# Modulation's sums on VectorE, k outermost in two first projections, and the residual's rows spread over the first expert

## The chip, the cores and the metric

The kernel runs on one core of a Trainium2 chip. The metric is the device time of one execution in microseconds (us). A time is the median of a few runs. One execution was also taken with the hardware profiler; its trace gives the rows shown below.

The engines: TensorE (PE; PEld is its loading of weights), VectorE (DVE), ScalarE (ACT), GpSimd (POOL), and SyncE (SP), which here issues nearly all of the transfers.

## The reference

The program computes two layers over 256 latent tokens of width 1024, with 256 context tokens beside the first layer. Everything is in fp32.

```
mods = split(silu(c) @ ada_w[i] + ada_b[i], 6)            # 6 vectors of 1024 per layer: the modulation
u = h * (1 + mods[1]) + mods[0]
layer 0: y = [neighbourhood attention | bidirectional SSD] (u) @ w_out
layer 1: y = short gated convolution (u)
h = LayerNorm(alpha * h + mods[2] * y) * ln_g + ln_b
f = channel(h * (1 + mods[4]) + mods[3])                  # layer 0: dense SwiGLU, layer 1: top-2-of-8 experts
h = LayerNorm(alpha * h + mods[5] * f) * ln_g + ln_b
```

The six modulation vectors of a layer are one row times a 1024 x 6144 matrix: 4 MB of weights for each vector of 1024, and little arithmetic. For the context tokens only the first two vectors of layer 0 are used.

## The kernel before

**Stages.** The program goes through the scan's projections, the scan and the values, z and its gate, attention (eight pairs of heads), the mixer's output projection, a norm and a turn (transposes that make u by feature), the dense feed-forward (22 tiles of features, then its output projection), a norm and a turn, the short convolution (8 tiles, then its output projection), the routing, and the eight experts with a final norm. An instruction's place in its engine's queue is fixed when the program is built: a scheduler orders each queue from a simulated timeline and the priorities of the program's order. `pinned` and `issue_after` put an instruction no earlier than the one named.

**Weights.** Every large weight comes as tiles of 1 MB (`raw`, L122, issued by SP) into a ring of buffers, whose number differs by stage. A granule of 1024 columns is split (`split`, L81): ScalarE copies the high part to fp32r (`whi`), VectorE subtracts to get the low part (`wlo`). A product is three fp32r matmuls: high x high, high x low, low x high (`mm3`, L90; `rows3`, L1245). A ring buffer is free when both parts of its two granules are made.

**Modulation.** `ada` (L242) is a generator that makes one or two vectors: it loads the weights, multiplies them on TensorE with `csil` (silu of c and of c_ctx, padded to 32 columns) as the stationary operand, four matmuls side by side in column groups of 32 (L258, plain fp32, two passes each), adds the bias, and turns the rows into columns (`modT`) or sends them through DRAM to all partitions (`gate`). For two vectors at a time a load is one k tile of 2048 columns; for one it is two k tiles of 1024. `background` (L99) hangs such generators onto the loads of a stage: after each `every` loads of the stage, `raw` lets the first task make one step, which is one load and its matmuls. Which vectors run where, layer/vector:

- z, attention and the mixer's output projection: 0/2 and 0/3, 0/4 and 0/5, half of 1/0 and 1/1, a step for every load (20 loads)
- ahead of the first norm: the other half of 1/0 and 1/1 (4 loads, `LEFT`)
- feed-forward: 1/2 and 1/3, and a quarter of 1/4, a step for every second load (9 loads)
- ahead of the second norm: the rest of 1/4 (3 loads, `REST`)
- routing: 1/5

**First projections.** After a turn, `ffn` (L835) and `short_conv` (L849) run `proj_T` for one output after the other: for each of the 8 k tiles of u the three matmuls, then the next output. The turn makes the k tiles of u one by one on ScalarE and VectorE.

**The residual's rows.** `keep_residual` (L822) writes alpha * (n * ln_g + ln_b) into h in eight VectorE steps of 512 columns. In the experts all eight are traced at once after the first expert's first product (L1342). n lies in the buffer `last`, and that buffer is one of the eleven of the experts' ring (L1455), so the load that falls to it waits for the last of these steps.

Of the kernel before, what the change touches and what calls it, by code (L numbers as in the profile page):

```python
# [7 lines left out]
F32 = mybir.dt.float32  # L8
# [4 lines left out]
OP = mybir.AluOpType  # L13
# [33 lines left out]
ONACT = ((0, 1), (1, 1))  # L47
LEFT = 4
X32 = 2
# [4 lines left out]
class Kernel:  # L54
# [43 lines left out]

    def background(self, tasks, every):  # L99

        self.tasks, self.every, self.loads = tasks, every, 0

# [19 lines left out]
    def raw(self, src, kk, cols):  # L122
        r = self.raw_tile()
        if not self.inside:
            self.loads += 1
            if self.loads % self.every == 0:
                self.inside = True
                self.step()
                self.inside = False
        v = r[:, :kk * cols].rearrange("p (k c) -> p k c", k=kk)  # L130
        self.nc.sync.dma_start(v, src)
        return v
# [48 lines left out]
    def constants(self):  # L181
        nc, io = self.nc, self.io
        c = self.const
        self.pad(c, 32)
        self.pad(self.work, 160)
        self.ident = c.tile([P, P], F32, name="ident")
        make_identity(nc, self.ident)
        self.ones = self.work.tile([P, P], F32, name="ones", bufs=1)
        nc.vector.memset(self.ones, 1.0)
        self.eps = c.tile([P, 1], F32, name="eps")  # L190
        nc.vector.memset(self.eps, EPS)
        self.ada_memory(self.work, 512)
# [48 lines left out]

    def ada(self, layer, m0, n, gates=(), cols=True, pin=False):  # L242

# [5 lines left out]
        bv = io["ada_b"][layer:layer + 1, c0:c0 + 4 * c].rearrange("a (j n) -> (a j) n", j=4)  # L249
        for r in range(2):  # L250
            nc.gpsimd.dma_start(self.ada_bias[r:r + 97:32, :c], bv)
        pa = self.ada_bank()
        kk = 512 // c
        for k0 in range(0, KT, kk):
            r = self.raw(w[:, k0:k0 + kk, c0:c0 + 4 * c], kk, 4 * c)
            for k in range(kk):
                for j in range(4):
                    nc.tensor.matmul(pa[32 * j:32 * j + 32, :c], self.csil[:, k0 + k, :], r[:, k, j * c:(j + 1) * c],  # L258
                                     start=(k0 + k == 0), stop=(k0 + k == KT - 1), tile_position=(0, 32 * j))
            yield k0  # L260
        rows = self.ada_rows[:, :c]
        done = nc.vector.tensor_add(rows, pa[:, :c], self.ada_bias[:, :c])
        if pin:
            self.pinned(done)
        if cols:
            pt = self.tmp()
            ns = c // P
            for s in range(ns):
                nc.tensor.transpose(pt[:, s * P:(s + 1) * P], rows[:, s * P:(s + 1) * P], self.ident)
            pv = pt[:, :c].rearrange("p (s j x) -> p s j x", s=ns, x=32)  # L270
            for r in range(2):
                nc.vector.tensor_copy(
                    self.modT[layer][:, r, m0 * KT:(m0 + n) * KT].rearrange("p (j s) -> p j s", s=ns),
                    pv[:, :, :, r].rearrange("p s j -> p j s"))
        if gates:
            flat = self.dram.tile([4, c], F32, name=f"gates{layer}{m0}")
            nc.gpsimd.dma_start(flat, rows[0:97:32, :])
            for m, dst in gates:
                j = (m - m0) * 4 // n
                nc.gpsimd.dma_start(dst, flat[j:j + 4 // n, :].rearrange("j n -> (j n)").partition_broadcast(P))  # L280

    def steps(self, task, n):
# [6 lines left out]
    def ada_memory(self, pool, c):  # L289
        self.ada_bias = pool.tile([P, c], F32, name="ada_bias", bufs=1)  # L290
        self.nc.gpsimd.memset(self.ada_bias, 0.0)
        self.ada_rows = pool.tile([P, c], F32, name="ada_rows", bufs=1)


# [49 lines left out]
    def proj_T(self, out, w, uh, ul, n, ks=range(KT)):  # L344

        for k in ks:
            self.mm3(out[:, :n], w[0][:, k], w[1][:, k], uh[:, k, :n], ul[:, k, :n], k == 0, k == KT - 1)
        return out[:, :n]

    def proj_tok(self, w, c0, n):  # L350
# [471 lines left out]
    def keep_residual(self, n, gb, factor):  # L822

        stt = self.nc.vector.scalar_tensor_tensor
        for i in range(NTT):
            for h in range(2):
                c = slice(h * 512, (h + 1) * 512)
                r = self.h[:, i, c]
                self.pinned(stt(r, n[:, i, c], factor, gb[:, 0, c], op0=OP.mult, op1=OP.mult))
                yield  # L830
                self.pinned(stt(r, gb[:, 1, c], factor, r, op0=OP.mult, op1=OP.add))
                yield


    def ffn(self, uh, ul, hh, hl, first, later):  # L835
        nc, io = self.nc, self.io
        ws = [self.by_feature(self.kpn(io[v][0]), 0, FFN, (t,)) for v, t in zip(("ffn_w1", "ffn_w3"), first)]
        for f in range(NF):
            p = self.acc("pf")
            for j in range(2):  # L840
                self.proj_T(p[:, j * T:], next(ws[j]), uh, ul, T)
            s = self.fp.tile([P, T], F32, name="fs", bufs=2)
            nc.scalar.activation(s, p[:, :T], AF.Silu)
            nc.vector.tensor_mul(s, s, p[:, T:])
            self.split(hh[:, f, :], hl[:, f, :], s)
# [3 lines left out]
    def short_conv(self, uh, ul, mh, ml, first, later):  # L849
# [3 lines left out]
        for ft in range(KT):  # L853
            p = [self.acc("pg"), self.acc("pg2")]
            reg = [p[0][:, :T], p[0][:, T:], p[1][:, :T]]
            for j in range(3):
                self.proj_T(reg[j], next(ws[j]), uh, ul, T)
            ci = self.fp.tile([P, T + 2], F32, name="sci", bufs=2)
# [15 lines left out]
    def front(self):  # L874
# [59 lines left out]
        for g in range(GROUPS):  # L934
# [3 lines left out]
        gp = self.pool("gates")  # L938
        gates = gp.tile([P, 2, D], F32, name="gates")
        gate = [gates[:, j, :] for j in range(2)]  # L940
        odd = self.ada(1, 0, 2, pin=True)
        self.background([self.ada(0, 2, 2, ((2, gate[0]),)), self.ada(0, 4, 2, ((5, gate[1]),)),
                         islice(odd, KT - LEFT)], 1)
        self.sh, self.sl = two(self.pool("mixs"), "mixs", KT)
# [9 lines left out]
        for half in range(2):  # L954
# [3 lines left out]
            nc.gpsimd.affine_select(out=wv[:, NKC:], in_=wv[:, NKC:], compare_op=OP.is_ge, fill=NEG,  # L958
                                    base=GW + 6 - NKC, pattern=[[-1, GW - NKC]], channel_multiplier=-1)
        self.attention()  # L960
        self.ready(AF.Sqrt, self.al[:, KT - 1, 0:1].bitcast(F32))
# [19 lines left out]
        self.residual_norm(accs, gate[0], n, ALPHA)  # L981
# [16 lines left out]
        first = [self.raw(w[:, :, j * D:j * D + 256], KT, 256) for j in (1, 2, 0)]  # L998
        self.residual_norm(accs, gate[1], n, 1.0)
# [315 lines left out]
    def experts(self):  # L1315
# [13 lines left out]
        for e in range(NE):  # L1329
            wu = [self.kpn(w[e]) for w in (w1, w3)]  # L1330
            wd = self.kpn(w2[e])
            po, last, x = None, None, xs[e % 2]
            for c, (c0, n) in enumerate(CHUNKS):
                def turned():
# [102 lines left out]
    def back_end(self):  # L1437
# [98 lines left out]
```

## Time and profile before

| | us |
|---|---|
| median of 3 runs | 1754.14 |
| fastest and slowest run | 1754.04, 1754.82 |
| the profiled execution | 1753.65 |
| its span (first to last instruction) | 1751.9 |
| TensorE, VectorE, ScalarE, GpSimd busy in the span | 1705.1, 1383.1, 1133.0, 119.1 |
| HBM read | 503.39 MB |

How to read the rows in this document. A row of a stretch reads: from and to in us, its length, then busy us and instructions of each engine that has any (PE, PEld, DVE, ACT, POOL in this order), the granted clock of TensorE, the busy share of the transfer engines, and GB/s. A row of the timeline reads: start, length in us, engine, line, operation, what it writes and what it reads, its shape, and how many were merged. A row of a group reads: line, engine, operation, tiles, shapes, count, then busy us and mean ns of one, then the idle time of the engine just before these and what ended most of it. A row of waits reads: who waited, for whom, us in total, times, the longest. Matmuls are pipelined, so that each one's record is longer than the distance to the next one's start.

### The profile page before, as it was taken

Reading aid. Unit: us, or ns where it says so; the run is one execution under the profiler, and the core shown is the slowest. Engines: PE = TensorE matmul, PEld = TensorE weight load, DVE = VectorE, ACT = ScalarE, POOL = GpSimd, SP = SyncE. Lnnn points to the kernel's source line nnn. Section 1 sums busy time; section 2 is a strip of 40 time slices with the busy share of each in tenths; the row PEclk is TensorE's granted clock in tenths of the full one; section 3 lists DMA queues with packets and bytes.
Section 4 is the critical chain, followed back from the end, with each engine's and each line's share of the span. In section 5 each row is a group of like instructions: output and inputs, shape, how many; then the busy total and the mean of one; then the engine's idle time right before and its main releaser. Section 6 shows DMA issues by size and latency. Waiting matters only on the chain. (4 is left out here: it accounts for less than half of the span.)

```text
span 1751.9 us, 25551 instructions
## 1 busy us (share of the span) xinstructions
PE 1705.1 (97%) x9400; PEld 1399.4 (80%) x9400; DVE 1383.1 (79%) x1784; ACT 1133.0 (65%) x1523; POOL 119.1 (7%) x241
## 2 busy tenths in 40 slices
PE   7999999999999999989999999999999999999996
PEld 5788776666999879768888888888888888888884
DVE  3697665555655567789998899998998998988987
ACT  3578554444444444468778877778777777777764
POOL 2036612110000010000000000000000000000000
PEclk9999999999999999999999999999999999999998
DMA  9346475358877585689999999999999999999991
GB/s 327 113 130 137 160 244 171 115 215 314 286 257 254 186 286 185 223 322 380 370 358 366 348 360 380 369 347 349 358 363 360 365 359 353 342 379 374 354 353 49
DMA packets 195358, 506.25 MB, mean 289 GB/s; under 512 B 9244, under 2 KB 79152, under 8 KB 191132
## 3 DMA queue, kind: packets, MB, share of 16 engines
q1 hardware_dynamic: 191504, 496.02, 77.8%
q0 software_dynamic: 3408, 8.44, 2.1%
q8 instruction: 75, 1.23, 0.3%
q14 instruction: 55, 0.45, 0.1%
q10 hardware_dynamic: 316, 0.12, 0.0%
HBM read 503.39 MB, written 1.14 MB: 288 GB/s over the span
## 5 line engine op out<-in xcount | busy, mean ns | idle before, releaser
L88 DVE TENSOR_TENSOR wlo<-wraw,whi 128x1024 fp32r<-128x1024 f32 x834 | 980.6, 1220 | 212.1 <-ACT whi L85 187.8
L85 ACT CAST whi<-wraw 128x1024 fp32r<-128x1024 f32 x834 | 840.1, 1054 | 347.5 <-PE bank L1251 74.5
L1250 PE MATMUL bank<-whi,x 128*128 128x512 f32 x896 | 349.3, 390 | 4.5 <-ACT whi L85 4.5
L1251 PE MATMUL bank<-whi,x 128*128 128x512 f32 x896 | 348.7, 390 | 0.0
L1253 PE MATMUL bank<-wlo,x 128*128 128x512 f32 x896 | 284.7, 392 | 3.6 <-DVE wlo L88 3.5
L1253 PEld LDWEIGHTS bank<-wlo,x 128*128 128x128 f32 x896 | 166.8, 188 | 42.7 <-DVE wlo L88 8.6
L1250 PEld LDWEIGHTS bank<-whi,x 128*128 128x128 f32 x896 | 168.1, 188 | 40.3 <-ACT whi L85 5.6
L1251 PEld LDWEIGHTS bank<-whi,x 128*128 128x128 f32 x896 | 168.1, 188 | 34.9
L1251 PE MATMUL bank<-whi,htl 128*128 128x512 f32 x440 | 171.5, 390 | 0.0
L1250 PE MATMUL bank<-whi,hth 128*128 128x512 f32 x440 | 171.5, 390 | 0.0
L1253 PE MATMUL bank<-wlo,hth 128*128 128x512 f32 x440 | 138.0, 395 | 0.0
L96 PE MATMUL pf<-ful,whi 128*128 128x256 f32 x352 | 100.0, 284 | 1.4 <-DVE ful L88 1.4
L95 PE MATMUL pf<-fuh,whi 128*128 128x256 f32 x352 | 100.6, 286 | 0.4 <-ACT fuh L85 0.4
L97 PE MATMUL pf<-fuh,wlo 128*128 128x256 f32 x352 | 99.4, 283 | 0.0
L1251 PEld LDWEIGHTS bank<-whi,htl 128*128 128x128 f32 x440 | 82.6, 188 | 17.6
L1250 PEld LDWEIGHTS bank<-whi,hth 128*128 128x128 f32 x440 | 82.6, 188 | 17.6
L95 PE MATMUL acc<-uh,whi 128*128 128x512 f32 (+1 forms) x256 | 92.1, 366 | 3.0 <-ACT whi L85 3.0
L1253 PEld LDWEIGHTS bank<-wlo,hth 128*128 128x128 f32 x440 | 80.0, 188 | 14.4
L96 PE MATMUL acc<-ul,whi 128*128 128x512 f32 (+1 forms) x256 | 91.4, 357 | 0.0
L97 PE MATMUL acc<-uh,wlo 128*128 128x512 f32 (+1 forms) x256 | 90.3, 353 | 0.0
L85 ACT CAST hth<-bank 128x512 fp32r<-128x512 f32 x56 | 32.3, 590 | 64.9 <-PE bank L1253 54.4
L95 PEld LDWEIGHTS pf<-fuh,whi 128*128 128x128 f32 x352 | 67.4, 192 | 7.8 <-issue 5.9
(372 smaller groups left out, 2505.0 us busy)
## 6 DMA issues: line engine op xcount, KB each, us to landing
wraw<-in_moe_w_dram SPq DMA_DIRECT2D x336, 1024.0 KB, 7.2
wraw<-in_ada_w_dram SPq DMA_DIRECT2D x40, 1024.0 KB, 5.2
wraw<-in_ffn_w_dram SPq DMA_DIRECT2D x32, 1024.0 KB, 6.1
wraw<-in_even_w_in_dram SPq DMA_DIRECT2D x24, 1024.0 KB, 6.5
wraw<-in_sc_w_in_dram SPq DMA_DIRECT2D x12, 1024.0 KB, 7.9
wraw<-in_ada_w_dram SPq DMA_DIRECT2D x16, 512.0 KB, 7.3
wraw<-in_even_w_out_dram SPq DMA_DIRECT2D x8, 1024.0 KB, 12.7
rb<-cumd POOLq DMA_DIRECT2D x16, 256.0 KB, 6.3
```

The lines of the kernel that those rows point to most:

```text
L85: self.high = nc.scalar.copy(hi, src)
L88: return (eng or nc.vector).tensor_tensor(lo, src, hi.bitcast(F32), op=OP.subtract)
L95: mm(out, ah, bh, start=start, stop=False)
L96: mm(out, ah, bl, start=False, stop=False)
L97: mm(out, al, bh, start=False, stop=stop)
L1250: mm(p, ah, at(wh, b), start=start, stop=False)
L1251: mm(p, al, at(wh, b), start=False, stop=False)
L1253: mm(p, ah, at(wl, b), start=False, stop=stop)
```

## The change

Four edits.

1. `ada` gets a number `vec`: that many of a task's loads are summed on VectorE (`ada_add`: weights times the column of `csil`, one instruction for each k tile, into `ada_sum`), and one set of four matmuls with ones as the stationary operand sums over the partitions. Tasks are of one vector now. 0/2, 0/3 and 0/4 run wholly on VectorE, from the attention's fifth load on (`background(..., AHEAD, 4)`: a step for every load after four); 0/5 follows on TensorE ahead of the first norm and shares the tile `gate` with 0/2. 1/0, 1/1 and 1/2 run wholly on VectorE in the feed-forward, and of 1/4 the first load; they begin six loads later (`SKIP`). 1/3 runs on TensorE in the short convolution.
2. The bias comes into the row tile itself, in one transfer; only the row for c is turned into `modT`.
3. `proj_first`: for the first tiles of the feed-forward and of the short convolution the k tiles are the outer loop and the outputs the inner one, with both products of the high weights; the products of the low weights follow at the end. Each output has a bank of its own there.
4. `keep_residual` in the experts is a background task, a step for every third load of the first expert; the buffer `last` comes into the ring at the first expert's last chunk.

```diff
-    def background(self, tasks, every):
-        self.tasks, self.every, self.loads = tasks, every, 0
+    def background(self, tasks, every, skip=0):
+        self.tasks, self.every, self.loads = tasks, every, -skip
...
-            if self.loads % self.every == 0:
+            if self.loads > 0 and self.loads % self.every == 0:
...
-    def ada(self, layer, m0, n, gates=(), cols=True, pin=False):
+    def ada(self, layer, m0, n, gates=(), cols=True, pin=False, vec=0):
...
-        for r in range(2):
-            nc.gpsimd.dma_start(self.ada_bias[r:r + 97:32, :c], bv)
-        pa = self.ada_bank()
+        nc.gpsimd.dma_start(self.ada_rows[0:97:32, :c], bv)
         kk = 512 // c
-        for k0 in range(0, KT, kk):
+        ends, pa = KT // kk, None
+        for s in range(ends):
+            k0 = s * kk
             r = self.raw(w[:, k0:k0 + kk, c0:c0 + 4 * c], kk, 4 * c)
...
+            if s < vec:
+                for k in range(kk):
+                    for h in range(0, 4 * c, 1024):
+                        self.ada_add(slice(h, h + 1024), r[:, k, h:h + 1024], k0 + k)
+            if s >= vec - 1 and pa is None:
+                pa = self.ada_bank()
+                if vec:
+                    for j in range(4):
+                        nc.tensor.matmul(pa[32 * j:32 * j + 32, :c], self.ones[:, 0:32],
+                                         self.ada_sum[:, j * c:(j + 1) * c],
+                                         start=True, stop=(vec == ends), tile_position=(0, 32 * j))
+            if s >= vec:
+                for k in range(kk):
+                    for j in range(4):
+                        nc.tensor.matmul(pa[32 * j:32 * j + 32, :c], self.csil[:, k0 + k, :],
+                                         r[:, k, j * c:(j + 1) * c], start=(k0 + k == 0),
+                                         stop=(k0 + k == KT - 1), tile_position=(0, 32 * j))
             yield k0
...
+    def ada_add(self, cols, w, k):
+        acc, c = self.ada_sum[:, cols], self.csil[:, k, 0:1]
+        if k == 0:
+            self.nc.vector.tensor_scalar(acc, w, c, None, op0=OP.mult)
+        else:
+            self.nc.vector.scalar_tensor_tensor(acc, w, c, acc, op0=OP.mult, op1=OP.add)
...
+    def proj_first(self, outs, ws, uh, ul, n):
+        mm = self.nc.tensor.matmul
+        for k in range(KT):
+            for out, (wh, wl) in zip(outs, ws):
+                mm(out[:, :n], wh[:, k], uh[:, k, :n], start=(k == 0), stop=False)
+                last = mm(out[:, :n], wh[:, k], ul[:, k, :n], start=False, stop=False)
+        with self.tc.issue_after(last.ins):
+            for out, (wh, wl) in zip(outs, ws):
+                for k in range(KT):
+                    mm(out[:, :n], wl[:, k], uh[:, k, :n], start=False, stop=(k == KT - 1))
...
-        odd = self.ada(1, 0, 2, pin=True)
-        self.background([self.ada(0, 2, 2, ((2, gate[0]),)), self.ada(0, 4, 2, ((5, gate[1]),)),
-                         islice(odd, KT - LEFT)], 1)
...
+        self.background([self.ada(0, 2, 1, ((2, gate),), False, vec=4)] +
+                        [self.ada(0, m, 1, vec=4) for m in (3, 4)], AHEAD, 4)
         self.attention()
...
-        self.special = iter([more] * LEFT + [self.wraw] * NRAW)
-        self.steps(odd, LEFT)
+        self.special = iter([more] * 4 + [self.wraw] * NRAW)
+        second = self.ada(0, 5, 1, ((5, gate),), False, pin=True)
+        self.steps(second, 4)
...
+        self.background([second], 1)
+        self.drain()
...
-        rest = self.ada(1, 4, 1, pin=True)
-        self.background([odd, self.ada(1, 2, 2, ((2, gate1),)), islice(rest, 4 - REST)], RATE)
+        rest = self.ada(1, 4, 1, pin=True, vec=4 - REST)
+        self.background([self.ada(1, m, 1, vec=4) for m in (0, 1)] + [self.ada(1, 2, 1, ((2, gate1),), False, vec=4),
+                         islice(rest, 4 - REST)], RATE, SKIP)
...
-        self.background([rest], 2)
+        self.background([rest, self.ada(1, 3, 1)], 2)
...
+                if e == 0 and c == len(CHUNKS) - 1:
+                    self.drain()
+                    p = self.nraw % len(self.raws)
+                    self.raws, self.nraw = [self.last] + self.raws[p:] + self.raws[:p], 0
...
-                    for _ in self.keep_residual(self.n, self.rows, ALPHA):
-                        pass
+                    self.background([self.keep_residual(self.n, self.rows, ALPHA)], 3)
...
-        self.raws, self.nraw = self.ring[:-1] + [self.last] + self.ring[-1:], 0
+        self.raws, self.nraw = self.ring, 0
```

`AHEAD` is 1 and `SKIP` is 6. `gate` and `ada_sum` take the place of the two gates that were kept; the row tile is 256 columns wide instead of two tiles of 512.

More of the change, by code (lines that the diff above doesn't have):

```diff
@@ L47 @@
 ONACT = ((0, 1), (1, 1))
-LEFT = 4
+AHEAD = 1
+SKIP = 6
 X32 = 2
@@ L191, in constants @@
         nc.vector.memset(self.eps, EPS)
-        self.ada_memory(self.work, 512)
+        self.ada_memory(self.work, 256)
         self.ada_bank = lambda: self.ps.tile([P, 512], F32, name="pa", tag="ada", bufs=1)
@@ L249, in ada @@
         bv = io["ada_b"][layer:layer + 1, c0:c0 + 4 * c].rearrange("a (j n) -> (a j) n", j=4)
-        for r in range(2):
-            nc.gpsimd.dma_start(self.ada_bias[r:r + 97:32, :c], bv)
-        pa = self.ada_bank()
+        nc.gpsimd.dma_start(self.ada_rows[0:97:32, :c], bv)
         kk = 512 // c
-        for k0 in range(0, KT, kk):
+        ends, pa = KT // kk, None
+        for s in range(ends):
+            k0 = s * kk
             r = self.raw(w[:, k0:k0 + kk, c0:c0 + 4 * c], kk, 4 * c)
[L256 to L259, printed above, removed]
+            if s < vec:
[15 more added lines that the diff above has]
+                                         stop=(k0 + k == KT - 1), tile_position=(0, 32 * j))
             yield k0
         rows = self.ada_rows[:, :c]
-        done = nc.vector.tensor_add(rows, pa[:, :c], self.ada_bias[:, :c])
+        done = nc.vector.tensor_add(rows, pa[:, :c], rows)
         if pin:
@@ L270, in ada @@
             pv = pt[:, :c].rearrange("p (s j x) -> p s j x", s=ns, x=32)
[L271 to L274, printed above, removed]
+            nc.vector.tensor_copy(
+                self.modT[layer][:, 0, m0 * KT:(m0 + n) * KT].rearrange("p (j s) -> p j s", s=ns),
+                pv[:, :, :, 0].rearrange("p s j -> p j s"))
         if gates:
@@ L289, in ada_memory @@
     def ada_memory(self, pool, c):
-        self.ada_bias = pool.tile([P, c], F32, name="ada_bias", bufs=1)
-        self.nc.gpsimd.memset(self.ada_bias, 0.0)
         self.ada_rows = pool.tile([P, c], F32, name="ada_rows", bufs=1)
+        self.nc.gpsimd.memset(self.ada_rows, 0.0)
     def first_bias(self):
@@ L829, in keep_residual @@
                 self.pinned(stt(r, n[:, i, c], factor, gb[:, 0, c], op0=OP.mult, op1=OP.mult))
-                yield
+                yield i
                 self.pinned(stt(r, gb[:, 1, c], factor, r, op0=OP.mult, op1=OP.add))
-                yield
+                yield i
     def ffn(self, uh, ul, hh, hl, first, later):
@@ L839, in ffn @@
             p = self.acc("pf")
-            for j in range(2):
-                self.proj_T(p[:, j * T:], next(ws[j]), uh, ul, T)
+            if f == 0:
+                reg = [p[:, :T], self.acc("pf")[:, :T]]
+                self.proj_first(reg, [next(w) for w in ws], uh, ul, T)
+            else:
+                reg = [p[:, :T], p[:, T:]]
+                for j in range(2):
+                    self.proj_T(reg[j], next(ws[j]), uh, ul, T)
             s = self.fp.tile([P, T], F32, name="fs", bufs=2)
-            nc.scalar.activation(s, p[:, :T], AF.Silu)
-            nc.vector.tensor_mul(s, s, p[:, T:])
+            nc.scalar.activation(s, reg[0], AF.Silu)
+            nc.vector.tensor_mul(s, s, reg[1])
             self.split(hh[:, f, :], hl[:, f, :], s)
@@ L855, in short_conv @@
             reg = [p[0][:, :T], p[0][:, T:], p[1][:, :T]]
-            for j in range(3):
-                self.proj_T(reg[j], next(ws[j]), uh, ul, T)
+            if ft == 0:
+                reg[1] = self.acc("pg3")[:, :T]
+                self.proj_first(reg, [next(v) for v in ws], uh, ul, T)
+            else:
+                for j in range(3):
+                    self.proj_T(reg[j], next(ws[j]), uh, ul, T)
             ci = self.fp.tile([P, T + 2], F32, name="sci", bufs=2)
@@ L938, in front @@
         gp = self.pool("gates")
-        gates = gp.tile([P, 2, D], F32, name="gates")
-        gate = [gates[:, j, :] for j in range(2)]
-        odd = self.ada(1, 0, 2, pin=True)
-        self.background([self.ada(0, 2, 2, ((2, gate[0]),)), self.ada(0, 4, 2, ((5, gate[1]),)),
-                         islice(odd, KT - LEFT)], 1)
+        gate = gp.tile([P, D], F32, name="gates")
+        self.ada_sum = gp.tile([P, D], F32, name="ada_sum")
         self.sh, self.sl = two(self.pool("mixs"), "mixs", KT)
@@ L980, in front @@
         f2 = self.f2 = self.pool("f2")
-        self.residual_norm(accs, gate[0], n, ALPHA)
+        self.residual_norm(accs, gate, n, ALPHA)
+        self.background([second], 1)
+        self.drain()
         self.turn(n, self.affine(self.small, 0, 0, 0, 4, 3), uh, ul)
@@ L998, in front @@
         first = [self.raw(w[:, :, j * D:j * D + 256], KT, 256) for j in (1, 2, 0)]
-        self.residual_norm(accs, gate[1], n, 1.0)
+        self.residual_norm(accs, gate, n, 1.0)
         self.turn(n, self.affine(self.small, 0, 1, 1, 1, 0), uh, ul)
         gb = self.norm_rows(0, 1, fp.tile([P, 2, D], F32, name="rows", bufs=1))
-        self.background([rest], 2)
+        self.background([rest, self.ada(1, 3, 1)], 2)
         self.close("more")
@@ L1333, in experts @@
             for c, (c0, n) in enumerate(CHUNKS):
+                if e == 0 and c == len(CHUNKS) - 1:
+                    self.drain()
+                    p = self.nraw % len(self.raws)
+                    self.raws, self.nraw = [self.last] + self.raws[p:] + self.raws[:p], 0
                 def turned():
```

## The prediction

> **What bounds the kernel now.** I read the page's busy shares first, then the busy time of every engine in one stretch per stage, then TensorE's waits in the stretches that are not full. (A change of 0.2%, 3.5 us, is about what a measurement of this kernel can tell from none.)
>
> ```profile
> PE 1705.1 (97%) x9400; PEld 1399.4 (80%) x9400; DVE 1383.1 (79%) x1784; ACT 1133.0 (65%) x1523; POOL 119.1 (7%) x241
> ```
>
> TensorE is busy 97% of the span, but a share says nothing of the stages. The stages (span in us, then PE, PEld, DVE, ACT and, if used, POOL busy in it):
>
> ```profile
> 190.00:240.00 50.00, 49.06 (x354) 39.21 (x353) 26.30 (x54) 25.98 (x54) 17.65 (x25) 1.00 0.67 228
> 240.00:376.00 136.00, 133.80 (x761) 87.66 (x759) 84.63 (x186) 69.35 (x143) 24.08 (x38) 1.00 0.49 164
> 376.00:425.00 49.00, 49.00 (x231) 37.36 (x230) 20.82 (x24) 17.45 (x19) 0.00 (x0) 1.00 0.88 339
> 425.00:432.00 7.00, 6.49 (x51) 2.69 (x49) 6.13 (x16) 4.73 (x9) 0.00 (x0) 1.00 0.01 2
> 432.00:573.00 141.00, 139.21 (x1143) 129.84 (x1144) 80.58 (x116) 62.54 (x95) 3.37 (x6) 1.00 0.78 266
> 640.00:712.00 72.00, 71.00 (x579) 69.97 (x580) 56.52 (x94) 32.42 (x48) 3.21 (x16) 1.00 0.70 245
> 750.00:785.00 35.00, 27.98 (x125) 21.31 (x123) 29.07 (x46) 24.10 (x35) 0.58 (x1) 1.00 0.84 302
> 785.00:1700.00 915.00, 913.86 (x4188) 757.35 (x4189) 840.89 (x832) 705.88 (x810) 0.00 (x0) 1.00 0.97 362
> ```
>
> The stretches are: scan's end and z (190 to 240), attention (240 to 376), the mixer's output projection (376 to 425), its norm (425 to 432), the feed-forward's first half (432 to 573), the short convolution (640 to 712), the start of the experts (750 to 785) and the rest of them. TensorE is full in all but the norm and the start of the experts, at full clock; VectorE is idle for 51 us in attention, 28 in the output projection and 60 in the feed-forward. So in the front TensorE's order is the path: an instruction taken off it shortens the program by its length, unless the next wait takes its place. The experts after 785 keep their length, since nothing of their TensorE work changes; everything ahead of them moves them bodily.
>
> **The modulation's matmuls (L258).** TensorE's busy time for these alone, in the same stretches:
>
> ```profile
> 190.00:240.00 50.00, 8.26 (x48) 1.31 (x48) 1.00 0.67 228
> 240.00:376.00 136.00, 12.55 (x88) 2.00 (x88) 1.00 0.49 164
> 376.00:425.00 49.00, 2.99 (x24) 0.57 (x24) 1.00 0.88 339
> 425.00:432.00 7.00, 3.85 (x32) 0.83 (x32) 1.00 0.01 2
> 432.00:573.00 141.00, 9.59 (x80) 1.67 (x80) 1.00 0.78 266
> ```
>
> A load of the two-vector tasks is 8 records (four matmuls, two passes each). So 6 + 11 + 3 = 20 loads sit ahead of 425, four in the norm's shadow, and nine in the feed-forward (8 loads of 8, one of 16 half as wide). One visit, its successor, and a visit of two loads:
>
> ```profile
> 293.46 1.07 PE L258 MATMUL pa<-wraw,csil 128*32 128x512 f32 x8
> 294.46 0.66 PE L693 MATMUL pt<-ident,e 128*128 128x128 f32 x4
> ...
> 275.37 1.92 PE L258 MATMUL pa<-wraw,csil 128*32 128x512 f32 x16
> 277.22 0.66 PE L693 MATMUL pt<-ident,e 128*128 128x128 f32 x4
> ...
> 551.75 1.07 PE L258 MATMUL pa<-wraw,csil 128*32 128x256 f32 x16
> ```
>
> A load alone costs 294.46 - 293.46 = 1.00 us, two together 1.85: about 0.85 a load and 0.15 a visit. The rows count 1.07 for 1.00, so the 20 loads hold 23.8 less about 20 x 0.07 = 22.4 us of the path. Attention also waits for such loads to land:
>
> ```profile
> PE pa L258 <- DMA wraw<-in_ada_w_dram: 1.9, 2, 1.1
> ```
>
> *Removed ahead of 425:* all 20 go (12 loads, three vectors, now summed on VectorE; one vector, 0/5, follows in the norm's shadow; 1/0 and 1/1 move to the feed-forward). Up to 22.4 + 1.9 us. *Added:* per vector one matmul with ones: half of the 551.75 visit, 0.85 / 2 + 0.15, about 0.55 us, three times: 1.65. Net at most 22.6. I keep 1.6 back, most of the 1.9, because the sums can wait for the same transfers: **-21**. The lower end is half of that (rival 1).
>
> [...]
>
> *VectorE's side.* Each load is two sums of 1024 columns. Prices: four splits of 1024 in a row, all splits of the program, and VectorE's groups in 245 to 383 with the idle time before them:
>
> ```profile
> 759.85 4.62 DVE L88 TENSOR_TENSOR wlo<-wraw,whi 128x1024 fp32r<-128x1024 f32 x4
> ...
> L88 DVE TENSOR_TENSOR wlo<-wraw,whi 128x1024 fp32r<-128x1024 f32 x834 | 980.6, 1220 | 212.1 <-ACT whi L85 187.8
> ...
> L675 DVE TENSOR_TENSOR s<-s,bias 128x256 f32<-128x256 f32 x32 | 13.6, 427 | 13.4 <-PE s L671 13.3
> L88 DVE TENSOR_TENSOR wlo<-wraw,whi 128x1024 fp32r<-128x1024 f32 x17 | 20.8, 1225 | 18.6 <-ACT whi L85 16.4 <-ACT mixah L85 1.4
> L623 DVE TENSOR_SCALAR u<-tmp,vecT 128x256 f32<-128x256 f32 x8 | 3.9, 481 | 19.2 <-PE tmp L621 19.2
> ```
>
> Two tensors in, one out, 1024 columns: 1.14 us in a row of four. 24 sums ahead of 425 are 27 us, of which four loads (9 us) fall in attention, by the loads' order, and the rest in the projection. VectorE's idle time there is spent behind TensorE (13.3 and 19.2) and behind ScalarE's high parts; the sums fit into 51 and 28 us. Behind a sum that waits for its load on VectorE stand the softmax's add, maximum and scaling and the low parts; TensorE has the next pair's projections queued ahead of the transposes that need them. I cost this at nothing; if the gaps are not where the sums fall, it is rival 1.
>
> *Queues.* SP: the 8 loads of the projection carry 8 modulation loads as before; scan and attention carry 8 fewer (4 in place of 12), four of them returning in the feed-forward and four in the short convolution; the total stays at 40. A load's buffer now waits for two sums instead of a matmul. POOL: one bias transfer for two, but it now waits until the rows of the vector before have been turned or stored; behind it stand attention's bias rows, which are fetched a pair ahead. Nothing taken for either.
>
> *Feed-forward.* 9.59 less 9 x 0.07 = 9.0 us off TensorE, four ones on (2.2): **-6.8**. VectorE gains 26 sums, 30 us, against 60 idle up to 573 and more behind; the two-per-load rate leaves the transfers under what 376 to 425 carries.
> *Norm's shadow.* Four loads before, four after (3.85 us in a gap where VectorE is busy 6.1 of 7): nothing. Completing vector 0/5 puts one 256-column add (about 0.4 us) next to the turn: inside the noise.
> *Short convolution.* Vector 1/3 now runs there on TensorE, four loads at 1.00 in a full stage: **+4.0**.
>
> **k outermost in two first projections.** TensorE there waits for VectorE's low parts of u and ScalarE's high parts; the rows are of 425 to 440 and of 633 to 648, and a pair showing the pitch of a 256-column matmul:
>
> ```profile
> PE pf L96 <- DVE ful L88: 1.4, 2, 0.9
> PE pf L95 <- ACT fuh L85: 0.4, 1, 0.4
> ...
> PE pg L96 <- DVE ful L88: 0.9, 2, 0.6
> PE pg L95 <- ACT fuh L85: 0.4, 1, 0.4
> ...
> 438.51 0.28 PE L97 MATMUL pf<-fuh,wlo 128*128 128x256 f32 x1
> 438.63 0.28 PE L95 MATMUL pf<-fuh,whi 128*128 128x256 f32 x1
> ```
>
> The pitch is 0.12. After the last k tile is ready, the old order has 2 + 24 matmuls left in the feed-forward (3.1 us) and 2 + 48 in the convolution (6.0); the new one 4 + 16 (2.4) and 6 + 24 (3.6). That gives 0.7 and 2.4; the waits shown bound them at 1.8 and 1.3 together with smaller ones. I take **-2.5** for both, with 0 and -5 as ends.
>
> **The residual's rows over the first expert.** In 750 to 785 TensorE is idle 35 - 28 = 7.0 us, VectorE busy 29 of 35:
>
> ```profile
> PE bank L1250 <- ACT whi L85: 2.6, 2, 1.6
> PE bank L1253 <- DVE wlo L88: 2.5, 2, 1.3
> ...
> 750.00:785.00 35.00, 0.00 (x0) 0.00 (x0) 5.22 (x8) 0.00 (x0) 1.00 0.84 302
> ...
> 783.93 2.00 ACT L85 CAST whi<-wraw 128x1024 fp32r<-128x1024 f32 x2 [1.48 <-DMA wraw<-in_moe_w_dram]
> 785.02 0.50 PE L1250 MATMUL bank<-whi,x 128*128 128x512 f32 x1 [1.87 <-ACT whi L85]
> ...
> SPq L131 <- DVE hl L829: 1.9, 1, 1.9
> ```
>
> The third row is the residual's eight steps, 5.22 us. At one for three loads some three stay in this stretch, so VectorE gets 3 us back; the wait for low parts (2.5) should mostly go. The last three rows are one event: a load into the buffer that holds the residual's rows waits for the last of these steps, lands late, and TensorE stands 1.87 us. That buffer leaves the ring until the last chunk, so this goes too. The 2.6 for ScalarE's high parts stays. The five steps that move past 785 meet VectorE at 841 of 915; 3 us fit. **-3.5**; ends +3 (all five steps and a ring shorter by one buffer show on TensorE) and -7.0 (all idle time goes).
>
> **Sum.** -21 - 6.8 + 4.0 - 2.5 - 3.5 = -29.8. The profiled execution took 1753.65 us (span 1751.9, 1.75 around it), the median is 1754.14, 0.5 above: 1753.65 - 29.8 = 1723.9, forecast **1724**.
>
> **Rivals.**
> 1. *Half of what leaves TensorE in the front comes back as waits.* The order of each queue is fixed beforehand; a sum placed ahead of a softmax step or a low part waits for a transfer, and the 1.9 us wait for such loads shows that they do come late. For: VectorE has 85 of 136 us in attention already. Against: only four of the twelve loads fall there. -21 and -6.8 become -10.5 and -3.4: 1753.65 - 15.9 = 1738.
> 2. *More than forecast:* all of the 1.9, both starts at their ends and all 7.0 of the experts' start: -22.6 - 6.8 + 4 - 5 - 7 = -37: 1716.
> 3. *Slower: VectorE takes TensorE's place.* If every sum (50 x 1.14 = 57 us) stood on the path in attention, projection and feed-forward, the time would be 1753.65 - 29.8 + 57 = 1781. It decides from 30 of the 57 us on, that is when more than half of the sums' time shows as TensorE idle. Against: 139 us of VectorE idle in these stretches. [...] In attention, where GpSimd is busy 24 us, the subtractions with two inputs average 1225 ns (row L88), against 1220 over the program, so I give it nothing more.
> 4. *It does nothing:* the freed time is idle again in the same stages, because the transfers set the pace. Against: they are busy 0.49 of attention. 1754.
>
> **How the numbers follow.** Forecast 0.52, rival 1 0.25, rival 2 0.13, rival 3 0.06, rival 4 0.04. From 1713 to 1742 holds the first three with 3 to 4 us for each term's rounding; outside are 0.10 and some of the tails. Faster by over 0.2%: 0.90; within: 0.04; slower: 0.06.
>
> **What would show it.** Right: L258 records in the scan and attention stretches are gone, attention's period per pair is about 1 us shorter, TensorE still full with VectorE some 65 to 70% busy; the feed-forward is 6 to 7 us and the experts' first 35 us 3 us shorter; the convolution 2 longer. Wrong: TensorE waits in attention or projection for e, for low parts, or for the ones' sums; SP waiting for sums; new waits in the first expert for a buffer.

## The result, and the profile after

The changed kernel takes **1740.15 us** (median of 4 runs, 1739.33 to 1741.66), the kernel before 1754.09 (4 runs): ratio 0.9921, 95% interval 0.9907 to 0.9934. The forecast was 1724: the sign is right and the time lies inside the range, but the gain is 14 us where 30 were forecast.

The profiled execution of the changed kernel spans 1738.7 us. Its page and its busy times by stage (columns as before: stretch, length, then PE, PEld, DVE, ACT and POOL busy, granted clock, DMA share, GB/s) read:

```profile
PE 1687.2 (97%) x9306; PEld 1400.9 (81%) x9306; DVE 1436.4 (83%) x1834; ACT 1132.2 (65%) x1523; POOL 122.9 (7%) x239
```

```profile
240.20:372.70 132.50, 126.83 (x679) 87.00 (x678) 96.66 (x186) 65.17 (x139) 26.40 (x34) 0.96 0.43 138
372.70:419.20 46.50, 43.46 (x183) 34.41 (x182) 27.38 (x29) 16.53 (x18) 0.00 (x0) 0.93 0.92 339
425.80:556.50 130.70, 129.32 (x1067) 127.69 (x1068) 96.51 (x124) 62.90 (x96) 1.67 (x3) 1.00 0.82 280
625.20:700.60 75.40, 74.84 (x646) 71.64 (x645) 57.16 (x93) 32.29 (x48) 2.64 (x15) 1.00 0.82 292
738.90:772.50 33.60, 29.50 (x129) 22.48 (x128) 27.78 (x43) 28.17 (x38) 0.59 (x1) 1.00 0.83 300
```

Two rows are not like the others. In attention (first) and in the output projection (second) TensorE is less full than it was: 5.7 and 3.0 us idle, where the kernel before has 2.2 and none. And the column behind POOL, the granted clock, is 0.96 and 0.93, where every stage of the kernel before had 1.00.

The length of each stage, worked out from the first and last TensorE instruction of each, in the profiles of the two kernels and of four of the experiments below:

| stage, us | before | after | e8 | e15 | e17 | e16 |
|---|---|---|---|---|---|---|
| start to the first dt matmul | 48.5 | 50.7 | 50.6 | 49.8 | 51.3 | 49.8 |
| from there to the first scores | 196.7 | 189.5 | 189.7 | 189.7 | 189.4 | 189.4 |
| attention | 137.6 | 132.5 | 128.3 | 130.7 | 127.2 | 135.4 |
| output projection | 42.5 | 46.5 | 46.2 | 39.2 | 39.3 | 43.8 |
| norm | 6.3 | 6.6 | 6.6 | 8.5 | 8.5 | 6.6 |
| feed-forward, first half | 141.6 | 130.7 | 130.7 | 130.1 | 130.1 | 130.8 |
| feed-forward, second half, norm | 66.0 | 68.7 | 68.7 | 68.7 | 68.7 | 68.7 |
| convolution to routing | 106.7 | 109.8 | 109.8 | 109.8 | 110.2 | 110.0 |
| experts | 1006.0 | 1003.7 | 1003.8 | 1000.1 | 999.9 | 1001.7 |

Scan and feed-forward did what they should. Attention gained 5 us and the projection lost 4. TensorE's waits from 240 to 420 us (us in all, times, longest) name the places:

```profile
PE pt L727 <- DVE e L716: 4.4, 2, 2.3
PE po L96 <- ACT whi L86: 2.3, 1, 2.3
```

The first is in attention's last pair. TensorE's order there, and VectorE's over the same time (start, length, last bracket: idle before it and its releaser):

```profile
355.08 0.60 PE L727 MATMUL pt<-ident,e 128*128 128x128 f32 x4
355.52 0.38 PE L283 MATMUL tmp<-ident,ada_rows 128*128 128x128 f32 x2
358.16 1.94 PE L727 MATMUL pt<-ident,e 128*128 128x128 f32 x8 [2.26 <-DVE e L716]
362.27 1.09 PE L727 MATMUL pt<-ident,e 128*128 128x128 f32 x4 [2.17 <-DVE e L716]
...
364.92 0.63 PE L97 MATMUL po<-wlo,mixsh 128*128 128x512 f32 x1
365.35 0.63 PE L98 MATMUL po<-whi,mixsl 128*128 128x512 f32 x1
```

```profile
354.40 0.48 DVE L716 TENSOR_SCALAR e<-e,m 128x512 f32<-128x512 f32 x1
354.79 0.75 DVE L299 TENSOR_SCALAR ada_sum<-wraw,csil 128x1024 f32<-128x1024 f32 x1
355.45 0.22 DVE L715 RECIPROCAL m<-m 128x1 f32<-128x1 f32 x2
355.59 1.27 DVE L301 SCALAR_TENSOR_TENSOR ada_sum<-wraw,csil,ada_sum 128x1024 f32<-128x1024 f32 x1
356.78 0.42 DVE L89 TENSOR_TENSOR mixal<-po,mixah 128x256 fp32r<-128x256 f32 x1
357.11 0.90 DVE L716 TENSOR_SCALAR e<-e,m 128x512 f32<-128x512 f32 x2
```

Two sums of vector 0/4's first load stand ahead of the scalings (L716) that TensorE waits for. They wait for no transfer themselves: VectorE has no gap there. In the kernel before, the same place was covered by modulation matmuls:

```profile
371.20 0.60 PE L269 MATMUL tmp<-ident,ada_rows 128*128 128x128 f32 x4
372.60 1.06 PE L258 MATMUL pa<-wraw,csil 128*32 128x512 f32 x8 [0.80 <-DMA wraw<-in_ada_w_dram]
373.60 1.09 PE L693 MATMUL pt<-ident,e 128*128 128x128 f32 x8
```

And the stall costs twice. The two projection matmuls at 364.92 and 365.35 take 0.63 us and start 0.43 apart; at 394 us the same kind takes 0.39 and starts 0.23 apart. The granted clock in stretches of 3.4 us around both stalls (behind PE and PEld stand DVE, ACT, POOL, then the clock):

```profile
354.30:357.70 3.40, 1.60 (x10) 0.86 (x8) 3.40 (x9) 1.63 (x4) 1.43 (x7) 1.00 0.01 1
357.70:361.10 3.40, 1.94 (x8) 1.57 (x8) 2.14 (x6) 1.82 (x4) 0.04 (x1) 0.50 0.86 284
361.10:364.50 3.40, 2.23 (x7) 1.18 (x8) 0.65 (x2) 0.89 (x3) 0.00 (x0) 0.50 0.09 30
364.50:367.90 3.40, 3.40 (x8) 2.64 (x9) 0.00 (x0) 0.00 (x0) 0.00 (x0) 0.50 0.00 0
...
395.20:398.70 3.50, 1.14 (x4) 0.30 (x2) 3.43 (x4) 1.90 (x2) 0.00 (x0) 0.99 1.00 321
398.70:402.10 3.40, 2.71 (x6) 2.15 (x7) 3.40 (x4) 2.00 (x3) 0.00 (x0) 0.50 1.02 319
402.10:405.50 3.40, 3.40 (x9) 2.64 (x8) 3.40 (x4) 1.05 (x1) 0.00 (x0) 0.50 0.92 331
405.50:408.90 3.40, 3.40 (x16) 2.82 (x15) 2.23 (x3) 1.05 (x1) 0.00 (x0) 1.00 1.06 339
```

After a stretch in which TensorE was busy 1.60 (1.14) of 3.4 us, the clock is half for 10.2 (6.8) us. TensorE's 7.6 and 6.1 busy us at half clock would take about 0.23/0.43 of that at full clock: some 3.5 and 2.8 us lost (an estimate) besides the stalls' own 4.4 and 3.0 (2.29 and the 0.75 behind it).

How many sums run in attention is to be read from the trace and not from the order of the loads. The sums alone, in attention (length, then PE, PEld and DVE busy):

```profile
240.20:372.70 132.50, 1.28 (x16) 0.32 (x16) 19.38 (x16) 0.96 0.43 138
```

With two more ahead of 240 us, 18 of the 24 sums, those of nine of the twelve loads, are done when attention ends; six are left for the projection.

From this came theory T: the front's missing gain is (1) the stall in the last pair, (2) the stall in the projection, (3) the half clock after each, (4) 2.2 us at the start, where one load of attention goes ahead of the first modulation's last two on SP. The rival R: VectorE's sums as such are the path there.

### The profile page after: what moved, and what is told of

It reads as the page before. It is cut to its first block, busy times and chain, and to the rows that moved or that the text cites. A ratio compares the mean times of both kernels' runs of the same rounds, so it can differ in the third digit from the quotient of the medians.

```text
span 1738.7 us, 25434 instructions
## 1 busy us (share of the span) xinstructions
PE 1687.2 (97%) x9306; PEld 1400.9 (81%) x9306; DVE 1436.4 (83%) x1834; ACT 1132.2 (65%) x1523; POOL 122.9 (7%) x239
## 5 line engine op out<-in xcount | busy, mean ns | idle before, releaser
L96 PE MATMUL pf<-fuh,whi 128*128 128x256 f32 x336 | 95.4, 284 | 0.0
L98 PE MATMUL pf<-fuh,wlo 128*128 128x256 f32 x336 | 95.1, 283 | 0.0
L97 PE MATMUL pf<-ful,whi 128*128 128x256 f32 x336 | 95.1, 283 | 0.0
```

Source lines behind the costliest of these rows:

```text
L96: mm(out, ah, bh, start=start, stop=False)
L97: mm(out, ah, bl, start=False, stop=False)
L98: mm(out, al, bh, start=False, stop=stop)
```

## The experiments

All times are medians; each ratio is against executions of the kernel before on the same chip (its medians were 1754.3, 1755.0, 1755.7 and 1753.5 on the four chips used). Each variant has one profile. `...` marks what is left out of code.

**e1: the start's order.** In `raw`, every load behind the first modulation's last transfer:

```
+        d = self.nc.sync.dma_start(v, src)
+        if self.mod_last is not None:
+            self.behind(d, self.mod_last)
...
```

> The changed kernel, with every weight load queued on SP behind the first modulation's last transfer (in the changed kernel one attention load goes ahead of the last two at 32.0 us). Theory T (three by-products eat the front's gain: the start's order 2.2 us, stalls of TensorE at 356 to 362 us and 395 to 399 us, and the half clock that is granted after each): all stages from 50 us on come 2.2 us earlier, 1738 us. Theory R (VectorE's sums as such are the path of attention and projection, and by-products only move waits): the start gains 2 us, which is lost again before 425 us, 1740 us.

1739.44 us, ratio 0.9915 (0.9901 to 0.9930): no gain. The first dt matmul still starts at 50.6 us. In the 14 profiles it starts between 48.5 and 51.3 us, at 50.8 in e6, which has the start of the kernel before. Part (4) of T falls: the profile of before, at 48.5, has the earliest start of all, and the 2.2 us are no work of the change.

**e8: two sums moved.** In `ada_add`, and after `attention()`:

```
+            first = self.nc.vector.tensor_scalar(acc, w, c, None, op0=OP.mult)
...
+                if self.firsts == 2:
+                    self.behind(first, self.last_scale)
...
+        self.last_scale = self.scaled
```

`scaled` is attention's last scaling.

> The changed kernel, with the two sums of vector 0/4's first load put behind the last softmax scaling of attention on VectorE; no other instruction moves. T: of the 4.4 us of stalls in attention's last pair about 1.8 stay, in pieces under 2 us, the clock is not halved there, attention ends 6 us earlier (2.7 of stall and about 3.7 of clock), and the projection's transfers, which start when attention ends, move with it: 1734 us. If the stalls go and the clock still halves: 2.7 us, 1737.5. R: the sums come later and the projection waits for them instead: 1740 us.

1735.69 us, ratio 0.9893 (0.9879 to 0.9908): 4.5 us less than the changed kernel, 6 forecast. TensorE's last pair and the clock:

```profile
356.45 1.06 PE L731 MATMUL pt<-ident,e 128*128 128x128 f32 x8 [0.84 <-DVE e L720]
359.25 0.65 PE L731 MATMUL pt<-ident,e 128*128 128x128 f32 x4 [1.73 <-DVE e L720]
```

```profile
356.30:359.70 3.40, 1.52 (x12) 1.28 (x12) 2.65 (x8) 2.12 (x5) 0.88 (x7) 1.00 0.01 1
359.70:363.10 3.40, 3.40 (x9) 2.11 (x8) 1.34 (x2) 0.58 (x1) 0.00 (x0) 0.50 0.12 37
363.10:366.50 3.40, 3.40 (x16) 2.63 (x14) 0.45 (x1) 1.05 (x1) 0.00 (x0) 1.00 0.72 276
```

The stalls went from 4.43 to 2.57 us. My limit of 2 us was an estimate (the kernel before has full clock behind a gap of 1.87 us, the changed kernel half clock behind one of 2.26), and it was too high: behind a gap of 1.73, with one of 0.84 ahead of it, 3.4 us of half clock still follow. The two sums were 1.9 of the 4.4 us; the other 2.6 are the softmax's own time, which nothing covers any more (with the modulation's matmuls back, in e2 below, such waits come to 0.8 us in all of attention). R is not borne out here: the sums came later, and nothing waited for them; the projection is 46.2 us long, 46.5 before this edit.

**e4: the stall filled, its cause left.** 14 transposes of the identity into a spare bank ahead of each of the last pair's first two groups; the groups of that pair are pinned to their order on TensorE as well.

> The changed kernel, with 2 x 14 additional transposes of the identity into a spare bank on TensorE in attention's last pair, one group ahead of each of the first two groups of transposes of the softmax (added work, its result unused). It fills the stalls and leaves their causes. T (idle time halves the clock): no half clock at 357 us, and the stage ends up to 3.7 us earlier although TensorE has 4.6 us more to do: 1736.5 to 1738 us. A clock that halves for another reason (power, VectorE's or the transfers' load) halves again, and the time is 1740 to 1742.

1735.37 us, ratio 0.9888 (0.9873 to 0.9902), a little better than expected.

```profile
356.80 1.75 PE L730 MATMUL fill<-ident 128*128 128x128 f32 x14
358.38 0.60 PE L732 MATMUL pt<-ident,e 128*128 128x128 f32 x4
358.82 1.69 PE L730 MATMUL fill<-ident 128*128 128x128 f32 x14
360.35 1.04 PE L732 MATMUL pt<-ident,e 128*128 128x128 f32 x8
```

The clock is 1.00 from 350 to 370 us. Without the added transposes 2.3 of the 3.4 us from 356.2 to 359.6 would have been idle. So at this place, in this profile, the half clock went with TensorE's idle time, and not with the load on VectorE or on the transfers, which the edit leaves alone. The median is 4.8 us below the changed kernel's. The profile doesn't place all of that: in it attention is only 0.8 us shorter, 131.7 us, since 6.8 us of half clock fell at 250 us, where the changed kernel's profile has none.

**e10: h on another queue.** `nc.gpsimd.dma_start(self.h, xv)`.

> The changed kernel, with the load of the residual rows h, which waits for attention's end and behind which SP's queue stands from 357 to 373 us, on GpSimd's queue. T: modulation and projection loads start as buffers come free, the transfers are spread over 360 to 410 us, the stall of 3 us at 395 to 399 and the half clock after it go: 1734 to 1736 us. If the buffers, and not h, hold the loads: the same times as before this edit, 1740 us. R: 1740 us too, with TensorE waiting for VectorE in the projection.

1739.0 us, ratio 0.9910 (0.9895 to 0.9924). SP now gets one load further and stands again until attention's last product:

```profile
357.67 0.37 SPq L132 DMA_DIRECT2D wraw<-in_ada_w_dram  x1
372.11 0.37 SPq L132 DMA_DIRECT2D wraw<-in_even_w_out_dram  x1
```

```profile
SPq L132 <- PE po L734: 14.0, 1, 14.0
```

The buffers, which lie in memory that attention gives back, hold the loads, not h alone. The projection was 2.3 us shorter in the profile, the wait in its middle still 2.0, now for a low part.

**e13: the modulation loads from attention's first load on.** With e8's edit (last scaling ahead of vector 0/4's first sums), `AHEAD, 0` for `AHEAD, 4`.

> The changed kernel with attention's last scaling ahead of vector 0/4's first sums (as in the run with that alone, 1735.7 us), and in addition the modulation loads from attention's first load on and not from its fifth: eight in attention, four in the projection. Theory T2 (the projection's stall comes from the transfers, saturated from 380 to 410 us, and the half clock from the stall): four loads fewer there, no wait of over 1 us for a projection load and no half clock at 390 to 400 us, the projection 42 to 43 us long instead of 46.2: 1731 to 1732 us. Theory R (VectorE's sums are the path): attention, which now holds twice the sums, gets longer by up to 8 x 1.2 = 10 us, the projection shorter by less: 1736 us or more.

1747.17 us, ratio 0.9954 (0.9941 to 0.9968): 11 us worse than e8, so T2 as I put it is wrong. Modulation loads issued early push the projection's own loads back; five of these now come after attention where three do in e8, and ScalarE's high parts wait for them, four times:

```profile
ACT whi L86 <- DMA wraw<-in_even_w_out_dram: 24.4, 4, 11.9
```

Attention is 135.6 us, 7.3 longer than in e8, as long as R said, but not for R's reason: it holds 14 sums (17.9 us) where e8 has 16 (19.4), since eight of e13's ran before it. What grew is TensorE's idle time, 7.4 us for 3.5, and the half clock, 10.2 us for 3.4. The largest part is one gap of 3.6 us at 253 us, in the first pair, where sums stand between the steps of the softmax; 6.8 us of half clock go with it. The edit also put work of vector 0/5 into the projection (36 more modulation matmuls than in e8), so that it is no clean test of how many loads share the transfers. It points at which loads come first; e15 tests that.

**e15: the projection's loads first.** With e8's edit; h's load and `norm_rows`' loads (2 MB, used only by the norm and behind it) queued behind the projection's eight:

```
-        nc.sync.dma_start(self.h, xv)
...
+        hl = nc.sync.dma_start(self.h, xv)
+        for d in self.outer[-8:]:
+            self.behind(hl, d)
+        self.rows_behind = hl
```

> The changed kernel with attention's last scaling ahead of vector 0/4's first sums (alone 1735.7 us), and with the residual rows h and the feed-forward's norm rows (2 MB) queued behind the output projection's eight loads on SP and not among them. Theory T3 (what the transfers deliver first after attention's end sets the projection's stall: 2 MB at 400 GB/s are 5 us ahead of the load that TensorE waits for): the wait for a high part at the projection's middle goes from 2.4 us to under 1, no half clock follows, the projection takes 42 to 43 us instead of 46.2: 1731 us. Rival: the transfers are saturated to 410 us whatever their order, and h and the modulation loads are late at the norm instead: 1735 us or more.

**1728.44 us**, ratio 0.9852 (0.9839 to 0.9866). SP's order after attention in the changed kernel, then in e15:

```profile
372.75 0.37 SPq L1012 DMA_DIRECT2D h<-in_x_dram  x1
...
375.56 2.83 SPq L852 DMA_DIRECT2D rows<-in_ln_g_dram  x1
378.43 0.58 SPq L852 DMA_DIRECT2D rows<-in_ln_b_dram  x1
...
381.67 0.51 SPq L132 DMA_DIRECT2D wraw<-in_even_w_out_dram  x1
```

```profile
370.29 0.37 SPq L132 DMA_DIRECT2D wraw<-in_even_w_out_dram  x1
...
379.16 0.37 SPq L132 DMA_DIRECT2D wraw<-in_even_w_out_dram  x1
379.57 0.51 SPq L1026 DMA_DIRECT2D h<-in_x_dram  x1
```

```profile
370.20:409.40 39.20, 39.20 (x177) 32.19 (x180) 25.43 (x26) 16.60 (x17) 0.00 (x0) 1.00 0.98 371
```

The projection is full, at full clock, and 39.2 us long, 7.0 less than in e8 with transfers no less busy (0.98; 0.92 in the changed kernel). The norm gives 1.9 back, since vector 0/4's end falls into it, and attention 2.4, with 6.8 us of half clock for 3.4 at the same stall of 1.73 us and 1.1 us of waiting for k where e8 has 0.2. The experts are 3.7 us shorter than in e8: e8's profile has 3.4 us of half clock at 742 us, where e15's has none; their start was also ordered anew by the scheduler, and the rest was not taken apart.

**e16: the same order, no sums ahead of the feed-forward.** `vec=0` for 0/2 to 0/4; and **e2**, the same in the changed kernel.

> The same order of the transfers, with vectors 0/2 to 0/4 on TensorE (12 loads of 0.85 to 1.0 us, no sums on VectorE ahead of the feed-forward). If the sums are worth their matmuls once the two stalls are gone: 9 us slower than the run of this call with the sums, 1740 us, and no half clock in either. If VectorE's sums cost as much as they take from TensorE wherever the stalls lie: the same time as that run.

> The changed kernel with vectors 0/2 to 0/4 back on TensorE at the places they have (no sums on VectorE ahead of the feed-forward, nothing else edited). T: TensorE gets 12 loads of 0.85 to 1.0 us and loses three visits of ones of 0.57, +9; the stalls in attention's last pair are filled by these matmuls and the clock is not halved there, -8; the projection's stall stays: 1740 to 1742 us, so that the sums as built earn about nothing ahead of 425 us. If the sums do earn their matmuls as forecast: 1749 us.

e16: 1738.48 us, 0.9910 (0.9897 to 0.9924); e2: 1738.92, 0.9910 (0.9895 to 0.9925). So the sums earn nothing as the change places them (e2 against 1740.15) and 10 us once the two places are mended (e16 against e15). e2 has full clock from 25 to 1720 us and no wait over 0.5 us in the projection: its TensorE is slower by the matmuls and does not run ahead of the transfers. ScalarE waits as long for the projection's late load as in the changed kernel, 11.2 and 11.0 us, and with the matmuls back that reaches TensorE no more. So the new order of the transfers earns nothing without the sums (e16 against e2).

**e17: ten transposes in the one stall left.** e15, with a filler in the 1.7 us wait ahead of attention's last group.

> The kernel of the run with h and the norm rows behind the projection's loads (1728.4 us), with ten additional transposes of the identity (added work of some 1.1 us, result unused) in the one wait that is left in attention's last pair, 1.7 us ahead of its last group of transposes; there the profile showed 6.8 us of half clock after it. If TensorE's idle share in that stretch sets the clock: no half clock at 355 to 366 us, attention shorter by about 3 us at the same wait for the softmax, 1725.5 us. If the clock follows something else: half clock again and 1728.5 us. The added work cannot gain anything in another way, since the wait it stands in ends with the scaling on VectorE.

1726.01 us, ratio 0.9847 (0.9834 to 0.9861).

```profile
358.26 1.25 PE L736 MATMUL fill<-ident 128*128 128x128 f32 x10
359.35 0.38 PE L286 MATMUL tmp<-ident,ada_rows 128*128 128x128 f32 x2
360.06 0.66 PE L738 MATMUL pt<-ident,e 128*128 128x128 f32 x4 [0.33 <-DVE e L723]
```

```profile
240.70:367.90 127.20, 124.43 (x689) 85.71 (x688) 96.49 (x186) 65.12 (x139) 27.95 (x34) 1.00 0.45 148
```

Attention has clock 1.00 and is 3.5 us shorter than in e15, with the transposes in it. That the transposes did this is not shown. The medians differ by 2.4 us and their intervals overlap, and one profile of each says little of the clock: behind the same gap of 1.73 us e8's profile has 3.4 us of half clock and e15's 6.8, and behind one of 1.87 us the kernel before has none. What speaks for the transposes is the mean granted clock, 0.991 to 0.993 in e15's five executions and 0.993 to 0.996 in e17's; being a mean of the whole execution it names no place. This is the lowest median of all.

**e6, e7, e18: the other parts, on the kernel before.** e6 has `proj_first` alone, e7 the residual's rows over the first expert alone, e18 both.

> The kernel before, with k tiles outermost in the two first projections alone. The record: 0.7 us in the feed-forward and 2.4 in the short convolution, -2.5: 1751.5 us. Rival: the waits shown bound it, and the later activation of the feed-forward's second bank gives it back: 1754 us.

> The kernel before, with the residual's rows spread over the first expert (one step for three loads, their buffer in the ring from the last chunk on) alone. The record: -3.5 us, mostly TensorE's waits for low parts in the first 35 us of the experts and the stand at the ring's buffer: 1750.5 us. Rival, from the changed kernel's trace (its first expert's start to the first 33 us +1.5, behind that -3.9): -2.4, 1751.7 us. Rival: the steps only move, 1754 us.

> The kernel before, with k tiles outermost in the first projections and the residual's rows over the first expert, without any change of the modulation. Alone they gave +3 us (TensorE stood 7 us at 783 for a load into the buffer of the residual's rows) and -3.6 us. If that stand is the buffer's, it is gone with the rows over the first expert, and k outermost gives its gain of the two stages (1.7 us): -5.3, 1749.5 us. If k outermost harms the experts' start in another way: 1751 to 1754 us.

e6: 1758.17 us, 1.0020 (1.0011 to 1.0029), slower; e7: 1751.44, 0.9980 (0.9971 to 0.9989); e18: 1748.68, 0.9964 (0.9950 to 0.9978). In e6's profile the two stages with `proj_first` are 0.8 and 0.9 us shorter, but TensorE stands in the experts for a load that comes late, and the clock is half for 10.2 us (785.8 to 796.0):

```profile
789.98 0.80 PE L1272 MATMUL bank<-whi,x 128*128 128x512 f32 x1 [6.97 <-ACT whi L85]
```

```profile
788.88 4.83 ACT L85 CAST whi<-wraw 128x1024 fp32r<-128x1024 f32 x5 [5.19 <-DMA wraw<-in_moe_w_dram]
```

It is the stand at the ring's buffer that the prediction saw at 785 us, 1.87 us there: the load goes out at 783.53, right behind the last step that reads the buffer (until 783.50; 777.24 in the kernel before), and lands at 788.86. Why the steps come later in e6 is open. With the rows over the first expert the stand is gone, and both parts together give 7.0 us: `proj_first` is a loss without the other edit. What it adds to that edit is less certain: the gains are 7.0 and 3.6 us, but the intervals of the two ratios overlap, so that only the lengths of the two stages show it.

## Why the prediction was wrong, point by point

**The front, -21: the step that failed.** From the first dt matmul to the projection's end the profiles show 376.8 us before and 368.5 after: -8.3. (All stages together give -13.2: +2.2 at the start, which is scatter, -8.3, +0.3 in the norm, -8.2 in the feed-forward, +3.1 in the convolution and -2.3 in the experts.) The failing sentences are those on VectorE's side, "TensorE has the next pair's projections queued ahead of the transposes that need them. I cost this at nothing", and on the queues, "Nothing taken for either". The first holds for seven pairs of eight; the last pair has no next projections, and its cover was the very matmuls that were taken away. The second took the projection's transfers as given because the number of loads stays 8; but TensorE, freed of the modulation, now arrives before its load, behind 2 MB that nobody needs yet. (The kernel before queues these 2 MB ahead of its last load too, and TensorE has no idle time in its projection.) The working priced both kinds of wait at their own length at most; that half clock comes with a stall (10.2 and 6.8 us of it here) was in none of its terms. The prediction named the sign of it: "TensorE waits in attention or projection for e, for low parts". One reading under it was wrong as well: "only four of the twelve loads fall there" went by the loads' order, and nine are summed before attention ends. It did little harm: in the changed kernel TensorE waits for the scalings in the last pair alone.

**Was the mechanism right?** With both stalls mended (e17) the same stretch takes 355.9 us, -20.9 (2.2 of it come back in the norm): nearly all of the -21 was there to be had, and more than half of it was lost in two places, by some 7 us of stalls and some 6 of half clock. Rival 1, half of the front's gain coming back as waits, 1738, has about the right size, but its reason holds only in part. The waits are in two places only, and no sum that waits for a transfer is behind the long ones: one is made of two sums that stand ahead of scalings and of cover that was taken away, the other of a late load of the projection's own weights. And the feed-forward lost nothing, where rival 1 had it lose half. Rival 3 is not supported: there is no general wait for the sums (e8), though where they stand can lengthen attention (the first pair in e13).

**Feed-forward, -6.8, with its share of the k tiles -0.7.** The profiles show -10.9 in the first half and +2.7 behind it, -8.2: right. **Short convolution, +4.0 and -2.4.** +3.1 for +1.6. e18's stage is 1.9 us shorter than before, so vector 1/3 costs about 109.8 - 104.8 = 5.0 there: mis-sized by 1. **k outermost, -2.5.** 0.8 and 0.9 to 1.9 in the two stages: right in size, but only with the residual edit. **Residual, -3.5.** e7 gives -3.6 (1751.44 against 1755.01): right, and for the reason given: in the experts' first 50 us TensorE's waits for high parts went from 4.5 to 2.5 us (the stand of 1.87 is gone) and those for low parts from 2.5 to 1.4. In the changed kernel the experts show -2.3. **Norm's shadow, nothing.** +0.3 in the changed kernel: right; +2.2 in e15 and e17.

## What to carry to other kernels

When matmuls are taken off a full TensorE, ask at each place where they stood which wait they covered; the last pass of a pipelined loop, with no next pass to fill it, is the first to look at, and the loads that come due when the engine arrives earlier are the second. Before a helper's work goes to a second engine, fix where each piece stands against the steps that the first engine waits for, and put loads needed later behind those needed now. And price a stall of TensorE like the ones here at its length plus what half clock may cost behind it: 3.4 to 10.2 us of half clock came with gaps of 1.73 to 6.97 us (e8, e15, e6 and the changed kernel), none with one of 1.87 in the kernel before.

## What the hardware showed

**Half clock came with stalls of TensorE, but not with each.** All half-clock spells between 26 and 1705 us in the 14 profiles are 3.4, 6.8 or 10.2 us long. The changed kernel's profile has two: 10.2 us from 357.7 us on, with the gaps of 2.26 and 2.17 us in attention's last pair, and 6.8 from 398.7 on, behind the gap of 2.29 at 396. Single gaps of 1.73 (e13, at 363 us) and 1.98 us (e10, at 396 us) had half clock behind them too. The kernel before has none behind its gap of 1.87 us at 783 us, and the changed kernel none behind its gaps of 1.51 at 743 and 1.65 at 750. The length of the idle time alone doesn't decide: 0.78 us of it ahead of 250 us had half clock behind it in e4 and in e1, and 1.75 at 758 us had none in e7; what else counts is open.

Nor is what follows the same for the same stall: the gap of 1.73 us in attention's last pair has 3.4 us of half clock behind it in e8's profile and 6.8 in e15's. The mean granted clock of 21 executions of the kernel before on one chip goes from 0.992 to 0.997.

**A little useless work can pay.** 28 transposes of fp32 data, 3.4 us, stand in waits of 4.4 us; in e4 the clock is 1.00 from 350 to 370 us, and the median of the kernel with them is 4.8 us lower.
